# A router on the residual, first rows by a 0/1 matrix, and expert weights with buffers of their own

## The chip, the cores and the metric

One core of a Trainium2 chip runs the kernel. The metric is the device time of one execution in microseconds (us).

## What is computed

A backbone of two layers over 512 latent and 256 context tokens, 1024 wide, all in float32. Each layer: modulated RMSNorm, one input projection, three token mixers side by side, an output projection and a gated residual; then a modulated RMSNorm and a channel mixer, in the first layer a SwiGLU, in the last one the two best of eight experts:

```python
x = x + g1 * out_l
hl2 = modulate(rmsnorm(x, norm2[l]), sh2, sc2)
x = x + g2 * channel_mixer(hl2, l, ...)
...
probs = jax.nn.softmax((h @ router).astype(F32), axis=-1)
top_p, top_i = lax.top_k(probs, TOP_K)
top_p = top_p / jnp.sum(top_p, axis=-1, keepdims=True)
...
for e in range(N_EXPERTS):
    out = out + comb[..., e:e + 1] * swiglu(h, wg[e], wu[e], wd[e])
```

## The kernel before

Large products run in split float32: an operand is the sum of two parts (`hi`, `lo`, made by ACT at L206 and DVE at L207), and a product is three matmuls (`mm3`, L214 to L216, or `mm3x`, L220 to L222). Activations have features on partitions: `x[i]` is a [128, 512] tile, features 128 i and on, tokens along the row.

The order of the work is a static one for every engine: a scheduler walks over the program, and each engine runs its list in that order, waiting on semaphores. DMAs are issued from the lists of SP (weights), ACT and POOL; what waits at the head of a list holds what is behind it. SBUF is given out from two ends (`pa`, `pb`); a buffer over memory that another one had waits for that one's last reader. PSUM is shared out by name in `banks`.

What the change touches, all in the last layer:
- `tail`: loads the residual `xr0` to `xr7`, the gain row `g2p` and the router on ACT's queue (L617 to L623), and projects in two pieces of 256 tokens, token tiles 1 and 2 first, then 0 and 3. In a piece there are eight groups of 24 products of 256 columns, one for each 128 features, with a 512 KB weight tile (`wout`, four buffers) each; DVE adds each to the residual (L646). Then `stats` (L289) takes the mean square with products of a column of ones (L305) and a square root on DVE (`rsq`, L238 to L245: 12 dependent operations), a diagonal matrix `dg` times ones spreads it over the partitions (L316, L321), and the normalised tokens `hh` are x times that (DVE, L655) plus the shift (ACT, L656). Two modulation rows (`mod_rows`, L264 to L267, L662, L663) give `g2row`.
- `moe` (L757): router products on `hh` (L793), `tokens`: transposes (L230) of `hh` to rows `tk` and their store to DRAM (L798), then `route` (L948): the two best experts (`m`, `one`, `sel`), running counts (`cum`, `pos`), the 0/1 matrix `eq` (L989: which token is which of expert 0's rows), a search of the first expert's tokens by products with it (L994, L995), then `slots`, every token's rows, which are scattered to `ids` in DRAM and read back as `idx` (L807, L813).
- `Expert`: `prep` gathers an expert's rows `xa`, `xb` from DRAM (L1120, L1128), transposes and splits them; `run` makes ten steps of an expert, each with four weight tiles (`wmg`, `wmd`) that `load` has got a step ahead. Transposes of the residual to token rows stand ahead of the first expert. The weights have four buffers in `moe`'s first part and seven after `close()` has given the residual's memory back.
- `Combine` (from L839): puts the experts' rows on the residual and does the last norm, whose gain row is `nfrow`.

```python
        with tc.issue_after(found.ins):
            ex.first = ex.load((0, 0, None), 0)
        with tc.issue_after(placed.ins):
            tokens(x, True)
        close()
        ...
        k.weights(e2, None, pb, 7)
```

Of the kernel before, what the change touches and what calls it, by code (L numbers as in the profile page):

```python
# [8 lines left out]
F32 = mybir.dt.float32  # L9
# [11 lines left out]
# by layer: solve steps to a pair of query tiles; the step that the tokens' q and k are loaded at; how far ahead of the rest  # L21
# the solve goes; pairs behind every second chunk; buffers of L; work on one engine or another
# [5 lines left out]
# ---------------------------------------------------------------- host layout  # L28

def constants():  # L30
# [20 lines left out]
    # rotary tables of the latents, tokens on partitions  # L51
# [22 lines left out]
# features of a head of attention: the first of every rotated pair, then the second  # L74
# [3 lines left out]
# columns with features on partitions (12 tiles of 128), and with tokens on partitions (3 groups)  # L78
# [56 lines left out]
# ---------------------------------------------------------------- kernel  # L135

class K:
    def __init__(self, es, tc, A, out, dbg=None):
# [23 lines left out]
        # tokens' inputs to the experts, the token of every row of an expert, the experts' rows  # L162
# [17 lines left out]
    def banks(self, es, **n):  # L180
        """PSUM buffers by use, until es closes; [128, 512], names in capitals twice that."""
# [16 lines left out]
    def split(self, raw, n=1024):  # L198
        """The two parts, each exact in float32r, that a float32 operand is the sum of."""
# [24 lines left out]
    def transposes(self, srcs, w=128, m=128, b="pt"):  # L224
        """srcs [m, w] each -> side by side in one PSUM tile [w, m]."""
# [7 lines left out]
    def rsq(self, pool, v, sh, scale, eps, out, tag):  # L233
        """out = 1 / sqrt(v scale + eps): a first guess from the bits, three Newton steps."""
# [12 lines left out]
    # -- the modulation vectors, d on partitions: modc[l][:, s, t] for s = latent, context  # L247
# [7 lines left out]
    def mod_rows(self, l, g, b):  # L255
        """512 of the modulation vectors' columns; latent in the first row of every 32, context in the second."""
# [23 lines left out]
    def gains(self, l, which):  # L280
        """norm gain times (1 + scale): [128, 2, 8]."""
# [7 lines left out]
    def stats(self, pool, x, segs):  # L289
        """1 / rms of the token columns of segs, on all partitions, one PSUM tile each."""  # L290
# [43 lines left out]
    def modnorm(self, pool, hh, hl, x, s, o, n, gain, modc, sh0):  # L334
        """h = x * rstd * gain + shift, in parts, columns o .. o + n of stream s."""
# [1502 lines left out]
```

## Time and profile before

| | |
|---|---|
| time, median of 3 runs | 2198.43 us (2196.98 to 2198.94) |
| the profiled execution's span | 2199.0 us |
| TensorE (PE) busy | 2051.8 us, 93% |
| VectorE (DVE) busy | 1398.2 us, 64% |
| ScalarE (ACT) busy | 1013.7 us, 46% |
| GpSimd (POOL) busy | 157.3 us, 7% |
| last projection, gapless products | 1508.73 to 1560.2 us |
| first product of expert 0 | 1601.48 us |

A view by lines or a timeline names an instruction by its line, engine and tiles (out<-in) and shapes; behind it, in brackets, stands the idle time of that engine just ahead of it and what ended it (`<-DMA raw<-wmg`: the arrival of a weight tile). PEld is the loading of stationary operands, which runs beside PE. A matmul of plain float32 is counted as two rows (x2), and as x4 for two of them. The view by stretches gives busy time, the share of full TensorE clock that was granted (PEclk) and the share and rate of the DMA engines.

### The profile page before, as it was taken

The page shows a single profiled execution, that of the slowest core. Times are in us where ns is not written, and L with a number is a line of the kernel's source. Part 1 is how long each engine was busy: PE and PEld are TensorE (multiplying, and loading weights), DVE is VectorE, ACT ScalarE, POOL GpSimd, SP SyncE. Part 2 cuts the span into 40 slices and gives each one's busy share as a digit, 9 for nine tenths or more (in the row PEclk, how much of TensorE's full clock was granted, in tenths as well). Part 3 has the DMA queues.
Part 4 walks back from the last instruction along what each step waited for, and adds up shares of the span by engine and source line. Part 5 has one row for each costly group of instructions (what it writes and reads, how often), then busy time and mean ns, then how long its engine had stood idle before and what let it go on. Part 6 is the DMA issues. An engine that isn't in the chain of part 4 may idle for free. (4 is left out here: it accounts for less than half of the span.)

```text
span 2199.0 us, 33960 instructions
## 1 busy us (share of the span) xinstructions
PE 2051.8 (93%) x12562; PEld 1647.8 (75%) x12562; DVE 1398.2 (64%) x2736; ACT 1013.7 (46%) x1771; POOL 157.3 (7%) x226
## 2 busy tenths in 40 slices
PE   6999999989999999999989997898889999999995
PEld 2988766776788888888859875677667777777774
DVE  4859967765442424242366599787667788766776
ACT  3664386633322222222235534763455576555554
POOL 0000201100000000000000003120020000000010
PEclk9999999999999999999999999999989999999998
DMA  6332544053432325131343323116497799667683
GB/s 260 96 119 65 169 162 159 30 190 103 151 111 86 116 82 216 34 98 58 96 170 113 105 75 108 40 30 208 178 262 277 240 349 343 208 234 234 241 286 127
DMA packets 120755, 342.48 MB, mean 156 GB/s; under 512 B 13104, under 2 KB 34592, under 8 KB 120576
## 3 DMA queue, kind: packets, MB, share of 16 engines
q1 hardware_dynamic: 80064, 271.75, 36.8%
q0 software_dynamic: 15248, 49.97, 6.7%
q10 hardware_dynamic: 25264, 18.42, 2.7%
q8 instruction: 107, 1.75, 0.3%
q14 instruction: 72, 0.59, 0.1%
HBM read 304.95 MB, written 35.14 MB: 155 GB/s over the span
## 5 line engine op out<-in xcount | busy, mean ns | idle before, releaser
L206 ACT ACTIVATE hi<-raw 128x1024 fp32r<-128x1024 f32 (+3 forms) x444 | 427.1, 987 | 350.6 <-PE ps L215 245.1
L207 DVE TENSOR_TENSOR lo<-raw,hi 128x1024 fp32r<-128x1024 f32 (+3 forms) x444 | 495.3, 1135 | 123.4 <-ACT hi L206 108.4
L214 PE MATMUL ps<-hh,hi 128*128 128x512 f32 (+1 forms) x1040 | 355.5, 342 | 0.5 <-ACT hi L206 0.5
L215 PE MATMUL ps<-hl,hi 128*128 128x512 f32 (+1 forms) x1040 | 354.9, 341 | 0.0
L216 PE MATMUL ps<-hh,lo 128*128 128x512 f32 (+1 forms) x1040 | 354.3, 341 | 0.0
L214 PEld LDWEIGHTS ps<-hh,hi 128*128 128x128 f32 x1040 | 197.4, 190 | 27.1 <-ACT gh L1226 2.5
L215 PEld LDWEIGHTS ps<-hl,hi 128*128 128x128 f32 x1040 | 197.3, 190 | 23.8
L216 PEld LDWEIGHTS ps<-hh,lo 128*128 128x128 f32 x1040 | 197.2, 190 | 23.6
L222 PE MATMUL ps<-lo,xh 128*128 128x512 f32 (+1 forms) x384 | 151.4, 395 | 8.3 <-DVE lo L207 5.1
L220 PE MATMUL ps<-hi,xh 128*128 128x512 f32 (+1 forms) x384 | 147.3, 384 | 3.6 <-ACT hi L206 3.2
L1225 DVE TENSOR_TENSOR sg<-sg,ps 128x512 f32<-128x512 f32 (+1 forms) x44 | 24.4, 555 | 197.1 <-PE ps L216 197.1
L221 PE MATMUL ps<-hi,xl 128*128 128x512 f32 (+1 forms) x384 | 145.7, 379 | 0.0
L215 PE MATMUL ps<-gl,hi 128*128 128x256 f32 (+1 forms) x352 | 119.6, 340 | 0.0
L214 PE MATMUL ps<-gh,hi 128*128 128x256 f32 (+1 forms) x352 | 119.1, 338 | 0.0
L216 PE MATMUL ps<-gh,lo 128*128 128x256 f32 (+1 forms) x352 | 118.6, 337 | 0.0
L222 PEld LDWEIGHTS ps<-lo,xh 128*128 128x128 f32 x384 | 73.1, 190 | 35.7 <-DVE lo L207 15.8
L739 DVE SCALAR_TENSOR_TENSOR xr<-ps,modc,xr 128x512 f32<-128x512 f32 (+1 forms) x80 | 49.4, 617 | 72.5 <-PE ps L216 72.4
L220 PE MATMUL ps<-hi,hh 128*128 128x400 f32 (+2 forms) x272 | 90.9, 335 | 2.9 <-ACT hi L206 2.7
L221 PE MATMUL ps<-hi,hl 128*128 128x400 f32 (+2 forms) x272 | 87.8, 324 | 0.0
L222 PE MATMUL ps<-lo,hh 128*128 128x400 f32 (+2 forms) x272 | 87.7, 326 | 0.0
L220 PEld LDWEIGHTS ps<-hi,xh 128*128 128x128 f32 x384 | 73.4, 191 | 17.6 <-ACT hi L206 4.6
L221 PEld LDWEIGHTS ps<-hi,xl 128*128 128x128 f32 x384 | 73.1, 190 | 14.6
(557 smaller groups left out, 4144.4 us busy)
## 6 DMA issues: line engine op xcount, KB each, us to landing
raw<-wmg SPq DMA_DIRECT2D x176, 512.0 KB, 5.5
raw<-wmod SPq DMA_DIRECT2D x96, 512.0 KB, 4.6
raw<-wmd SPq DMA_DIRECT2D x80, 512.0 KB, 4.8
raw<-wgu SPq DMA_DIRECT2D x44, 512.0 KB, 3.9
raw<-wout SPq DMA_DIRECT2D x32, 512.0 KB, 3.8
raw<-wt SPq DMA_DIRECT2D x24, 512.0 KB, 3.6
raw<-wd SPq DMA_DIRECT2D x32, 256.0 KB, 2.7
raw<-wd SPq DMA_DIRECT2D x16, 384.0 KB, 3.1
```

The source lines that it names most:

```text
L206: self.nc.scalar.activation(hi, src, AF.Copy)
L207: self.nc.vector.tensor_sub(lo, src, hi.bitcast(F32))
L214: mm(out, wh, xh, start=start, stop=False)
L215: mm(out, wh, xl, start=False, stop=False)
L216: mm(out, wl, xh, start=False, stop=stop)
L220: mm(out, xh, wh, start=start, stop=False)
L221: mm(out, xl, wh, start=False, stop=False)
L222: mm(out, xh, wl, start=False, stop=stop)
L739: nc.vector.scalar_tensor_tensor(x[d][:, o:o + n], p[:, :n], k.modc[l][:, s, 40 + d:41 + d], x[d][:, o:o + n], op0=OP.mult, op1=OP.add)
L1225: nc.vector.tensor_mul(s, s, pu)
```

## The change

- Router on the residual. The norm's factor is the same for all of a token's features, so the router is multiplied with the gain once (`rg`, L649), applied to the residual as each group of the projection is done (`sums`, L668), and scaled by the factor behind it (L700); the shift's share is a constant of eight numbers (`lc`), by eight matmuls with a [128, 1024] copy of the shift (L651, L655). The sums of squares are products of one column (L670) of squares that ACT makes. `sums(m - 1)` stands behind group m.
- First expert's rows by products. The 0/1 matrix is kept (in `xa`, L1037), and `place` (L1163) multiplies the token rows `tk` with it: 32 float32 products of 192 columns give expert 0's rows with features on partitions. Gathers for expert 0, their transposes and the search are gone.
- Expert weights own their buffers: seven tiles, and `g2p`, opened ahead of the residual's at the end `pb`; the first seven tiles are loaded in the first piece of the projection (L686). The residual's transposes, `close()` and the load of `nfrow` are done in step 1 of expert 0; the copy of `g2row` is gone; the token rows are stored from ACT's queue (L841).

The diff, cut to its core:

```diff
 def tail(k, l, cat, mix, ec):
+    if last:
+        wm, g2p = pb(ec2, "wm", 7), pb(ec2, "g2")
     hp = pb(eh, "hp2")
...
-    k.banks(eb, ps=6, pn=2)
+    if last:
+        k.banks(eb, ps=4, pn=2, pl=2)
+    else:
+        k.banks(eb, ps=6, pn=2)
...
+        if last:
+            router = np_.tile([128, 8, 32], F32, name="router", bufs=1)
+            nc.scalar.dma_start(router, A["router"])
...
+            nc.vector.tensor_mul(rg, router, gain[:, 0].unsqueeze(2).to_broadcast([128, 8, 32]))
+            nc.vector.tensor_copy(shb, k.modc[l][:, 0, 24:32].unsqueeze(2).to_broadcast([128, 8, 128]))
+            for i in range(8):
+                nc.tensor.matmul(p[:, 0:8], shb[:, i], router[:, i, 0:8], start=i == 0, stop=i == 7)
+            nc.vector.tensor_copy(lc, p[:, 0:8])
...
+            def sums(m):
+                xs = cut(x[m], o, n)
+                sq = np_.tile([128, 256], F32, name="sq", bufs=3)
+                nc.scalar.activation(like(sq, o), xs, AF.Square)
+                j = 32 * (m % 4)
+                nc.tensor.matmul(pl[j:j + 32, :256], rg[:, m, :], xs, start=m < 4, stop=m >= 4, tile_position=(0, j))
+                for t in range(2):
+                    nc.tensor.matmul(pq[:, t:t + 1], sq[:, t * 128:t * 128 + 128], k.C("ones")[:, 0:1], start=m == 0 and t == 0, stop=m == 7,
+                                     skip_group_check=True)
...
+                if last and m:
+                    sums(m - 1)
+                if last and o == MID and m % 2:
+                    for r in range(m - 1, min(m + 1, 7)):
+                        raws.append(wm.tile([128, 1024], F32, name="raw"))
+                        nc.sync.dma_start(raws[-1], A["wmg"][0, r])
...
-                rs, = k.stats(np_, x, [(o, n)])
+                sums(7)
+                nc.vector.tensor_copy(lt, pl[:, :256])
+                k.rsq(np_, pq[:, 0:2], [128, 2], 1.0 / 1024, EPS, ss, "s")
+                for t in range(2):
+                    nc.tensor.matmul(pl[:, 256 + 8 * t:264 + 8 * t], lt[:, t * 128:t * 128 + 128], k.C("fold8"), start=True, stop=True)
+                nc.vector.tensor_mul(lg[:, o], pl[:, 256:272].rearrange("p (t e) -> p t e", t=2), ss.unsqueeze(2).to_broadcast([128, 2, 8]))
+                nc.vector.tensor_add(lg[:, o], lg[:, o], lc.unsqueeze(1).to_broadcast([128, 2, 8]))
...
 def moe(k, l, x, hs, g2row, close, lg, wm, raws):
-        k.weights(es, 8, pa, 4)
+        k.wraw, k.whl = wm, [pa(es, "w" + x, 8) for x in "hl"]
...
-            for t in range(4):
+            for t in (1, 2, 0, 3):
...
-                    nc.tensor.matmul(pl[j:j + 32, :256], k.router[:, i, :], hs[i][:, o:o + 256], start=i < 4, stop=i >= 4,
-                                     tile_position=(0, j))
...
-                nc.sync.dma_start(k.ht[t * 128:t * 128 + 128], tk[:, t])
+                nc.scalar.dma_start(k.ht[t * 128:t * 128 + 128], tk[:, t])
...
             ex.first = ex.load((0, 0, None), 0)
-        with tc.issue_after(placed.ins):
-            tokens(x, True)
-        close()
+            ex.place(tk, eq)
...
+        def residual():
+            tokens(x, True)
+            close()
+            cb.open(pb(e2, "cb"))
...
+    def place(self, tk, eq):
+        for q in range(4):
+            p = k.psum("pt")
+            for i in range(2):
+                f = (2 * q + i) * 128
+                for t in range(4):
+                    nc.tensor.matmul(p[:, i * CAP:i * CAP + CAP], tk[:, t, f:f + 128], eq[:, t], start=t == 0, stop=t == 3)
+            pv, f = p[:, :2 * CAP].rearrange("p (a t) -> p a t", a=2), slice(2 * q, 2 * q + 2)
+            k.parts(pv[:, :, 0:MAIN], xh[:, f], xl[:, f])
+            k.parts(pv[:, :, MAIN:], xs[:, f, 0:TAIL], xs[:, f, TAIL:])
```

The order on PE at the start of the last projection, after the change; `shb` is the copied shift, `pg` and `R,L` belong to the recurrence that the projection's last inputs come from, cat2 and cat3 are inputs of the projection:

```order
L230 MATMUL pg<-cst,oacc 128x128 x4
L1849 MATMUL pg<-R,L 64x64 x4
L655 MATMUL pn<-router,shb 128x8 x8
L214 MATMUL ps<-cat2h,hi 128x256
L215 MATMUL ps<-cat2l,hi 128x256
L216 MATMUL ps<-cat2h,lo 128x256
L214 MATMUL ps<-cat3h,hi 128x256
```

The products with the router now stand between the recurrence and the projection's products on cat2; before, those came behind the recurrence at once.

PE inside the projection. Before, around a pair of sums of squares, in the second piece's first group:

```order
L216 MATMUL ps<-cat7h,lo 128x256
L214 MATMUL ps<-cat2h,hi 128x256
L215 MATMUL ps<-cat2l,hi 128x256
L305 MATMUL pn<-sq,cst 32x256 x2
L216 MATMUL ps<-cat2h,lo 128x256
L214 MATMUL ps<-cat3h,hi 128x256
L215 MATMUL ps<-cat3l,hi 128x256
```

After, at the end of a group in the first piece (`xr` are residual tiles, `rg` the router times the gain, `sq` squares):

```order
L215 MATMUL ps<-cat1l,hi 128x256
L216 MATMUL ps<-cat1h,lo 128x256
L668 MATMUL pl<-xr_14317,rg 32x256
L668 MATMUL pl<-xr_14319,rg 32x256
L668 MATMUL pl<-xr_14321,rg 32x256
L668 MATMUL pl<-xr_14323,rg 32x256
L214 MATMUL ps<-cat5h,hi 128x256
L215 MATMUL ps<-cat5l,hi 128x256
L216 MATMUL ps<-cat5h,lo 128x256
L668 MATMUL pl<-xr_14325,rg 32x256
L670 MATMUL pn<-cst,sq 128x1 x2
L214 MATMUL ps<-cat6h,hi 128x256
```

Products of router and residual now stand in both pieces, four in a row here and one alone further on, and one-column products with the squares behind them.

DVE from the 0/1 matrix on. Before, the splits of expert 0's weights (`lo`) begin behind the search (`first`):

```order
L995 CAST first<-ps 128x1
L996 CAST first<-ps 64x1
L1011 TENSOR_TENSOR ex_15241<-ex_15240 128x8
L1061 TENSOR_SCALAR p_15094<-p_15094 128x4
L1065 TENSOR_TENSOR p_15216<-one_15190,pw 128x4
L1011 TENSOR_TENSOR ex_15242<-ex_15241 128x8
L207 TENSOR_TENSOR lo<-raw,hi 128x1024
L1011 TENSOR_TENSOR acc<-ex_15242 128x8
L1066 TENSOR_TENSOR pt_15095<-pt_15095,p_15216 128x4
```

After, just ahead of the first part of expert 0's rows (`xl<-pt`), which frees a PSUM buffer of `place`:

```order
L207 TENSOR_TENSOR lo<-raw,hi 128x1024
L1063 SCALAR_TENSOR_TENSOR pos<-cst,pos 128x32
L1087 TENSOR_SCALAR jb<-jb 128x8
L207 TENSOR_TENSOR lo<-raw,hi 128x1024
L1066 TENSOR_TENSOR lgt<-one_15231,pos 128x32
L1093 CAST jobs<-jb 128x9
L207 TENSOR_TENSOR lo<-raw,hi 128x1024
L1067 TENSOR_REDUCE row_15291<-lgt 128x4
L207 TENSOR_TENSOR xl<-pt,xh 128x256
```

These are the last three of six weight splits that DVE does between the matrix and the first part of the rows.

## Rows read from the trace of the kernel before

**Rows 1.** The page, busy time (us, share of the span) of each engine.
```profile
PE 2051.8 (93%) x12562; PEld 1647.8 (75%) x12562; DVE 1398.2 (64%) x2736; ACT 1013.7 (46%) x1771; POOL 157.3 (7%) x226
```

**Rows 2.** Stretches: us, busy us by engine (instructions), PEclk, DMA share, GB/s.
```profile
1490.00:1510.00 20.00, 13.96 (x145) 11.65 (x141) 18.87 (x52) 7.02 (x15) 1.23 (x2) 0.83 0.95 310
...
1530.00:1560.00 30.00, 29.76 (x226) 26.26 (x225) 18.65 (x41) 11.50 (x19) 0.00 (x0) 1.00 0.42 138
...
1590.00:1602.00 12.00, 6.53 (x29) 4.73 (x29) 8.01 (x30) 2.79 (x5) 7.09 (x7) 0.58 0.71 115
...
1602.00:1624.00 22.00, 17.68 (x64) 12.24 (x65) 9.86 (x11) 10.20 (x13) 3.88 (x5) 0.84 0.88 203
```

**Rows 3.** Timeline of PE, an insert: start us, us, instruction.
```profile
1533.08 0.28 PE L215 MATMUL ps<-cat2l,hi 128*128 128x256 f32 x1
...
1533.29 0.62 PE L305 MATMUL pn<-sq,cst 128*32 128x256 f32 x4
...
1533.84 0.39 PE L216 MATMUL ps<-cat2h,lo 128*128 128x256 f32 x1
```

**Rows 4.** Timeline of PE, the search for expert 0's tokens.
```profile
1584.37 1.61 PE L994 MATMUL ps<-cst,eq 128*128 128x1 f32 x16 [0.80 <-DVE eq L989]
```

**Rows 5.** Timeline of ACT's queue and PE; DMA issues of 1486:1512, KB each, us to landing.
```profile
1501.45 0.44 ACTq L623 DMA_DIRECT2D router<-router  x1
...
1508.73 0.28 PE L214 MATMUL ps<-cat3h,hi 128*128 128x256 f32 x1
...
raw<-wout SPq DMA_DIRECT2D x7, 512.0 KB, 5.8
...
router<-router ACTq DMA_DIRECT2D x1, 128.0 KB, 5.7
```

**Rows 6.** Timeline of PE and DVE behind the projection's last product.
```profile
1559.98 0.28 PE L216 MATMUL ps<-cat5h,lo 128*128 128x256 f32 x1
...
1566.33 2.24 PE L264 MATMUL ps<-raw,sT 128*32 128x512 f32 x8 [0.26 <-DMA raw<-wmod]
...
1566.69 0.17 DVE L238 TENSOR_SCALAR rqxs<-ss 128x2 f32<-128x2 f32 x1
...
1569.06 0.42 DVE L316 TENSOR_TENSOR dg<-cst,ss 128x256 f32<-128x256 f32 x1
...
1570.34 3.22 DVE L655 SCALAR_TENSOR_TENSOR hh<-xr,gain,pn 128x256 f32<-128x256 f32 x8 [0.86 <-PE pn L321]
...
1573.91 0.69 DVE L663 TENSOR_TENSOR g2p<-g2p,ps 128x512 f32<-128x512 f32 x1 [0.35 <-PE ps L662]
...
1581.39 0.17 DVE L977 TENSOR_TENSOR cum<-cum,sel 128x8 f32<-128x8 f32 x1
...
1583.36 0.95 DVE L989 TENSOR_TENSOR eq<-cst,p 128x768 f32<-128x768 f32 x1
```

**Rows 7.** Timeline of PE: step 5 of expert 0, expert 2's first product, its step 5.
```profile
1642.57 0.28 PE L220 MATMUL ps<-hi,xh 128*128 128x256 f32 x1
...
1748.70 0.39 PE L220 MATMUL ps<-hi,xh 128*128 128x512 f32 x1
...
1780.17 0.28 PE L220 MATMUL ps<-hi,xh 128*128 128x256 f32 x1
```

**Rows 8.** Timeline of DVE, PE and ACT between the matrix and expert 0.
```profile
1586.49 1.22 DVE L207 TENSOR_TENSOR lo<-raw,hi 128x1024 fp32r<-128x1024 f32 x1
...
1594.55 0.17 DVE L1038 CAST slots<-od 128x4 int32<-128x4 f32 x1
...
1595.37 4.78 PE L230 MATMUL pt<-cst,xr 128*128 128x128 f32 x20 [6.13 <-DVE tk L784]
...
1609.42 2.24 ACT L206 ACTIVATE hi<-raw 128x1024 fp32r<-128x1024 f32 x2 [4.92 <-DMA raw<-wmg]
```

**Rows 9.** Timeline of POOL: index load and gather for expert 1.
```profile
1616.35 0.96 POOL L813 DMA_DIRECT2D idx<-ids  x1 [11.55 <-DMA ids<-tid,slots]
...
1625.21 1.02 POOL L1120 DMA_INDIRECT xa<-ex,idx  x1 [7.17 <-DVE gl L207]
```

More of the change, by code (lines that the diff above doesn't have):

```diff
@@ L787, in moe @@
             hp = pa(e1, "h3")
[L788 to L795 removed]
             tokens(hs, False)
             for t in range(4):
[L798 to L800 removed]
+                nc.scalar.dma_start(k.ht[t * 128:t * 128 + 128], tk[:, t])
+            routing = route(k, hp, lg, slots, pw, jobs, last, ex.tl("xa", [128, 1024])[:, :4 * CAP].rearrange("p (t c) -> p t c", t=4))
+            found, eq = next(routing)
             placed = next(routing)
@@ L814, in moe @@
             nc.gpsimd.dma_start(idx[:TAIL, 1], rows[MAIN:])
-            ex.idx = [(first[:, 0:1], first[:TAIL, 1:2])] + [(idx[:, 0, e:e + 1], idx[:TAIL, 1, e:e + 1]) for e in range(1, 8)]
+            ex.idx = [None] + [(idx[:, 0, e:e + 1], idx[:TAIL, 1, e:e + 1]) for e in range(1, 8)]
         k.tap("slots", slots)
@@ L820, in moe @@
             ex.first = ex.load((0, 0, None), 0)
-        with tc.issue_after(placed.ins):
-            tokens(x, True)
-        close()
+            ex.place(tk, eq)
         e2 = ExitStack()
         pb = pools(k, l)[1]
-        k.weights(e2, None, pb, 7)
-        cb = Combine(k, pb(e2, "cb"), ex, tk, slots, pw, nfrow)
+        def residual():
+            tokens(x, True)
+            close()
+            cb.open(pb(e2, "cb"))
+        cb = Combine(k, ex, tk, slots, pw)
         flags = nc.values_load(jobs[0:1, 8:9], min_val=0, max_val=256 * NJOBS + 255)
-        ex.run([(e, e * CAP, (flags & (1 << e)) > 0) for e in range(8)], {(6, 1): lambda: cb.gathers(0), (6, 8): lambda: cb.others(0), (7, 1): lambda: cb.gathers(1), (7, 8): lambda: cb.others(1),
+        ex.run([(e, e * CAP, (flags & (1 << e)) > 0) for e in range(8)], {(0, 1): residual, (6, 1): lambda: cb.gathers(0), (6, 8): lambda: cb.others(0), (7, 1): lambda: cb.gathers(1), (7, 8): lambda: cb.others(1),
                   (7, 2): lambda: cb.last(*last), (7, 6): cb.place}, cb)
@@ L945, in far, with route @@
         self.finish()
-def route(k, pool, lt, slots, pw, jobs, first, last):
+def route(k, pool, lg, slots, pw, jobs, last, eq):
     nc = k.nc
     T_ = lambda n, s: pool.tile(s, F32, name=n)
-    p = k.psum()
-    for t in range(4):
-        nc.tensor.matmul(p[:, t * 8:t * 8 + 8], lt[:, t * 128:t * 128 + 128], k.C("fold8"), start=True, stop=True)
     sh = [128, 4, 8]
     i8 = k.C("iota8").unsqueeze(1).to_broadcast(sh)
-    lg, tmp, w8 = T_("lg", sh), T_("lgt", sh), T_("lgw", sh)
-    nc.vector.tensor_copy(lg, p[:, :32].rearrange("p (t e) -> p t e", t=4))
+    tmp, w8 = T_("lgt", sh), T_("lgw", sh)
     nc.vector.tensor_scalar(w8, i8, -1.0, 8.0, op0=OP.mult, op1=OP.add)
@@ L1085, in run @@
         w, self.first = self.first or self.load(*work[0]), None
-        self.prep(*jobs[0])
-        after = None
+        if not self.placed:
+            self.prep(*jobs[0])
+        self.placed, after = False, None
         for i, (j, c) in enumerate(work):
@@ L1101, in load @@
         if c < 6:
-            return [k.weight(sel(k.A["wmg"])[4 * c + r]) for r in range(4 if c < 5 else 2)]
+            return [k.split(self.raws.pop(0)) if self.raws else k.weight(sel(k.A["wmg"])[4 * c + r]) for r in range(4 if c < 5 else 2)]
         h, f0 = (c - 6) // 2, 6 * (c % 2)
```

70 lines of the change are left out of this document (38 added, 32 removed).

## The prediction

> **What bounds the kernel now.** I read the page first: TensorE (PE) is busy for 93% of the 2199.0 us span, so only PE's idle stretches and PE work that is added or dropped can change the time [rows 1]. Then the table of stretches. In 1530 to 1560, the second half of the last output projection, PE works 29.76 of 30 us [rows 2]. Behind it lies the passage: in 1590 to 1602 PE is busy 6.53 of 12 us and in 1602 to 1624 17.68 of 22, with granted clocks of 0.58 and 0.84 of full speed, 1.2 GHz and 2.4 GHz mixed [rows 2]. There the waits are read one by one. A second loose place is the start of the projection, 1490 to 1510: PE 13.96 of 20 us, DMA share 0.95 [rows 2].
>
> All sums are against the profiled execution, 2199.0 us; the median of the three runs is 0.6 lower. I call 0.2% (4.4 us) what a measurement can tell from no change: 2194.0 to 2202.8.
>
> **1. Sums and router products in the projection's stream: +9.3.** The projection's products follow each other every 0.12 us. An inserted pair of sums of squares costs more than its duration: the product ahead starts at 1533.08, the next one at 1533.84, so 0.64 goes to the insert, 0.55 of it from the insert's own start [rows 3]. Before, the first piece holds six such inserts, 6 x 0.64 = 3.84, and the second none, its sums come after its last product. After, sixteen router products of 256 columns (L668) and sixteen pairs of one-column sums (L670) go there.
> - One router product: the nearest row is that insert, of 256 columns in f32 too, 0.55. The search of before has products of one column, 16 rows in 1.61 us, 0.10 each [rows 4]; a pair of sums is 4 such passes, 0.40 behind another insert, 0.55 alone with the break.
> - First piece: four router products run together (0.7: two neighbours' four rows share 0.62 in [rows 3]), four apart (2.2); of the sums four stand alone (2.2), four beside a router product (1.6), and the two fold products add 0.55: 7.25. Less 3.84: +3.4.
> - Second piece: six router products in the stream (3.3) and sums behind them (2.55): +5.85.
> Bounds: if the one-column sums vanish under weight loads, +3; if nothing shares a break, 16 x 0.64 + 16 x 0.40 - 3.84 = +13.
>
> The trace has 0.10 for a pass of one column [rows 4]. The Trainium skill (TensorE: Matmul & The Clock Gate, section "Wait — 56ns, not 53.3ns?") gives a floor of about 25 ns from one matmul's start to the next, however few the columns. By it, an estimate, the 64 passes would take 1.6 us instead of 6.4, and the sum would be 4.8 lower; the row stands against it, and I keep the row.
>
> **2. The start of the projection: +4.** Eight new products (L655), ahead of all but six of the first group's products, need the router in SBUF. Its load is the last of ten on ACT's queue: issued at 1501.45, 5.7 us to landing, 1507.2 [rows 5]. Before, products go gapless at full clock from 1508.73 [rows 5]. After, four loads of expert weights of 512 KB each are issued in the same stretch, where the DMA engines are already 0.95 busy at 310 GB/s: 2 MB more is up to 6.7 us for what queues with it. I take the router at 1509.5, the eight products (16 passes of 0.10, some at the lower clock) to 1511.3, four products to be caught up, and about 1 us for products at 1.2 GHz behind the longer idle time (0.83 is granted on the mean of 1490 to 1510 as it is [rows 2]): +4. Bounds: 0 (the load lands as before, its products beside others) to +8. Queued behind the router on ACT's queue is nothing of PE's; DVE's multiplication of router by gain waits for the same load and holds the cat1 tiles a little.
>
> **3. From the last product to the 0/1 matrix: -4.5.** Before: the last product starts at 1559.98 (ends 1560.2), the matrix is made at 1583.36 + 0.95 = 1584.3 [rows 6]: 24.1. After, on the same clock: residual update 0.6, square 0.4, then PE has five products of the modulation row (0.28 each of 8 in 2.24 [rows 6]) and one router product ahead of the last sums: 1562.6. The square root's chain, 1566.69 to 1569.03 before [rows 6], is 2.4: 1565.0. One row update (0.69 [rows 6], behind L715's 1.13) stands in front of the diagonal in DVE's order: 1566.3; diagonal 0.4, its product 0.7, so the normalised tokens start at 1568.2 instead of 1570.34 [rows 6]. The router's products on the normalised tokens, their copies, the fold and its wait are gone. But the second row update now stands ahead of the running counts on DVE, and it waits for PE behind the first transposes, and those for ACT's shift of the tokens with a weight split of 1.05 among them: about 1576, against 1581.39 for the counts before [rows 6]. From there to the matrix 2.9 as before, and 0.8 for handovers that I can't price: 1579.8. Bounds -6 to -3.
>
> **4. From the matrix to the first expert at full pace: -3.** Before, expert 0's step 5 begins at 1642.57; expert 2, undisturbed, takes 1780.17 - 1748.70 = 31.5 for the same five steps [rows 7], so expert 0 in effect began at 1611.1, 26.8 behind the matrix. In that time stand the search (1.61 [rows 4] and a wait), the gather, residual transposes held by DVE (PE idle 6.13 [rows 8]), and ACT waiting for expert weights, 4.92 [rows 8]. After: 32 products of 192 columns, 64 passes at 0.20 (0.27 for 256 columns, half of an insert), 12.9, but only two PSUM buffers take them, and DVE's order puts six splits of 1.22 [rows 8] ahead of the first part that frees one: the third group waits till 10.2, the fourth about 2, and PE is at full pace at 17.3. The 32 transposes of the residual (20 in 4.78 at the low clock [rows 8], so some 0.14 each at the full one, 4.5, and hops) now stand inside step 1 of expert 0: +5. About 1.5 for the lower clock after PE's idle 3 us. Together 23.8: -3. The weights wait is gone, seven tiles being loaded ahead. Bounds: -8 (splits overlap with the products, no low clock) to +3.
>
> Removed at no gain: the copy of the gain row on ACT (ACT has spare time there), the gathers for expert 0 on POOL. Moved at no cost: token rows from SP's queue to ACT's, the reading of nfrow.
>
> Sum: +9.3 + 4 - 4.5 - 3 = +5.8, a profile of 2204.8, a median of 2204.
>
> **Rivals.**
> *Faster.* The small products cost little, since weight loads and products overlap (PEld is 26.26 busy of 30 us beside PE's 29.76 [rows 2]): term 1 at +3; the router lands early, term 2 at +1; and expert 0 begins without the low clock, term 4 at -5: 3 + 1 - 4.5 - 5 = -5.5, a median of 2193. It decides when an insert costs under 0.3 us. For it: four rows share one 0.62 [rows 3]. Against: each insert of before costs 0.64. 0.23.
> *No change.* Term 2 at 0 and the rest as summed: +1.8, 2200. The projection's cost is as large as the passage's gain. 0.27.
> *Slower still: expert 1's rows come late.* DVE finds the slots at 1594.55 [rows 8], 10 us behind the matrix; the index load begins only at 1616.35 and the gather at 1625.21 [rows 9]. After, the slots come 15 behind the matrix while expert 0 starts earlier: some 8 us of slack go. If that reaches the gather, expert 1 waits about 5: 2209. 0.10.
> *The loads ahead are not ahead.* The seven tiles lie where the mixers' buffers lay; the first waits for their last reader and stands on SP's queue ahead of the third weight tile of the projection. If it is released only at 1508, that tile lands at 1514 (5.8 to landing [rows 5]), is split by 1516.5, and PE stalls some 3 us more: 2207. 0.08.
>
> **Numbers.** The forecast, slower by the sum, has 0.32; with the last two rivals slower is 0.50, same 0.27, faster 0.23. Eight in ten: the low end reaches past the faster rival to 2190, the high end takes in the upper bound of term 2 with the late gather, 2213. The forecast's own range is 2203 to 2209.
>
> **What would show it.** The projection from its first gapless product to its last should take 9 us longer, each L668 opening about 0.64. L655 should wait for the router's load until about 1509.5. The tokens' normalisation should start 8 us behind the last product, the matrix end 19.6 behind it. L1163's third group should wait for DVE, and ACT should wait for no expert weights in expert 0. Wrong if an insert costs a third of this, or if expert 0's step 5 is not 55 us behind the matrix, as 23.8 + 31.5 has it.

## The result and the profile after

The changed kernel takes 2211.23 us (median of 9 runs, 2204.26 to 2216.82), the kernel before beside it 2198.94 (9 runs, 2193.72 to 2206.78): a ratio of 1.0053 [1.0036, 1.0069], the 95% interval in brackets, so it is slower by 0.5%, some 12 us. That is inside the wide range given, on the side that had the larger chance, 7 us above the number and outside the forecast's own range, 2203 to 2209. The profiled execution took 2208.62, with a span of 2207.0.

The page's first row, as in [rows 1], shows the loss already: PE has 11.5 us more of busy time and just as high a share.

```profile
PE 2063.3 (93%) x12638; PEld 1665.1 (75%) x12638; DVE 1392.2 (63%) x2737; ACT 1014.1 (46%) x1781; POOL 156.4 (7%) x224
```

Two executions don't reach the last layer's end at the same time, so I set all traces on one mark ahead of everything that the change moves: the start of ACT's second copy of `W` in the last step of the recurrence. In the kernel after it is this row of ACT's timeline; in the kernel before the same copy (at its L1746) starts at 1490.82, 3.0 us later.

```profile
1487.82 0.38 ACT L1805 ACTIVATE W<-pg 128x256 f32<-128x256 f32 x1 [0.49 <-PE pg L1801]
```

From that mark (A) to the projection's last product (P), from there to the 0/1 matrix (M, its start), and on to step 5 of expert 0 (S):

| us | A to P | P to M | M to S | A to S | forecast |
|---|---|---|---|---|---|
| before | 69.2 | 23.4 | 59.2 | 151.8 | |
| after | 90.3 | 18.1 | 54.0 | 162.3 | |
| difference | +21.1 | -5.3 | -5.3 | +10.5 | +13.3, -4.5, -3 |

Behind S both need the same time (2199.0 - 1642.57 = 556.4 before, 2207.0 - 1650.09 = 556.9 after). So the whole result is made here: the passage gained more than forecast, and the way to the last product lost 8 us more.

Where those 8 us are, the view by stretches says. Its columns are those of [rows 2].

```profile
1490.00:1500.00 10.00, 6.05 (x65) 4.83 (x60) 8.89 (x28) 3.53 (x7) 1.24 (x2) 0.76 0.99 361
1500.00:1510.00 10.00, 3.18 (x16) 2.58 (x16) 4.95 (x13) 2.72 (x5) 0.00 (x0) 0.67 1.02 350
1510.00:1520.00 10.00, 9.17 (x48) 8.83 (x49) 3.20 (x9) 0.28 (x1) 0.00 (x0) 0.54 0.54 195
```

In 1500 to 1510 PE, DVE and ACT all stand for half the time or more, while the DMA engines are full; in 1510 to 1520 PE works at nearly half clock. The timelines of SP's list, ACT and its list, and PE there, in order of time:

```profile
1490.56 0.80 SPq L686 DMA_DIRECT2D raw<-wmg  x2
1496.65 1.84 SPq L686 DMA_DIRECT2D raw<-wmg  x2
1497.15 8.00 ACTq L621 DMA_DIRECT2D xr<-xres  x4
1506.14 0.34 ACTq L645 DMA_DIRECT2D router<-router  x1
1506.53 2.00 ACT L206 ACTIVATE hi<-raw 128x1024 fp32r<-128x1024 f32 x2 [8.76 <-DMA xr<-xres]
1510.83 3.58 PE L655 MATMUL pn<-router,shb 128*128 128x8 f32 x16 [5.67 <-DMA router<-router]
1515.05 0.41 PE L214 MATMUL ps<-cat3h,hi 128*128 128x256 f32 x1
```

Four expert weight tiles (2 MB) are issued between 1490 and 1499. On ACT's list the last four `xr` loads then take 8.00 us to issue. Narrower windows of the same timeline show them one by one:

```profile
1500.29 0.33 ACTq L621 DMA_DIRECT2D xr<-xres  x1
1502.87 0.33 ACTq L621 DMA_DIRECT2D xr<-xres  x1
1504.82 0.33 ACTq L621 DMA_DIRECT2D xr<-xres  x1
```

An issue by itself is 0.33 us; the rest is waiting ahead of it. By the trace's semaphore events, the loads on SP's and ACT's lists take turns on eight semaphores in this stretch, and a load waits until the one that had its semaphore before has landed. The last three `xr` loads and the router's load meet the semaphores of the first four `xr` loads. Those were issued from 1493.38 to 1495.41, and their last events come at 1500.27, 1502.84, 1504.80 and 1506.12, each 0.02 to 0.03 us ahead of the issue that waited: 6.9 to 10.7 us to land.

The router's load is issued at 1506.14, 4.7 later than in [rows 5] though this execution is 3 us ahead. ACT's own next work, the weight split, stands behind both and has waited 8.76, until an `xr` load landed. PE waits 5.67 for the router. Then the clock is half: L655's sixteen passes take 3.58, and the products follow each other every 0.21 until 1519. From A, the first product on cat3h comes 27.2 behind, against 17.9 before (1508.73 in [rows 5]): +9.3, and about 2 more until the clock is full. Of the 21.1 us that A to P is longer, 5 are idle time of PE (11.6 us against 6.5); the rest is PE's own work, some of it at half clock.

The inserts, on PE's timeline (the columns of [rows 3]): a router product alone, a pair of sums alone, and both together.

```profile
1561.84 0.28 PE L216 MATMUL ps<-cat5h,lo 128*128 128x256 f32 x1
1562.05 0.62 PE L668 MATMUL pl<-xr,rg 128*32 128x256 f32 x2
1562.60 0.38 PE L214 MATMUL ps<-cat6h,hi 128*128 128x256 f32 x1
...
1563.41 0.28 PE L214 MATMUL ps<-cat2h,hi 128*128 128x256 f32 x1
1563.54 0.50 PE L670 MATMUL pn<-cst,sq 128*128 128x1 f32 x4
1563.90 0.36 PE L215 MATMUL ps<-cat2l,hi 128*128 128x256 f32 x1
...
1569.95 0.28 PE L216 MATMUL ps<-cat5h,lo 128*128 128x256 f32 x1
1570.16 0.62 PE L668 MATMUL pl<-xr,rg 128*32 128x256 f32 x2
1570.71 0.61 PE L670 MATMUL pn<-cst,sq 128*128 128x1 f32 x4
1571.18 0.36 PE L214 MATMUL ps<-cat6h,hi 128*128 128x256 f32 x1
```

Start to start less one product's 0.12 they cost 0.64, 0.37 and 1.11. From cat3h to the last product the stream takes 63.0 us against 51.25: +11.8. Added up insert by insert from the trace's starts, the new ones take 13.8 us and those of before 4.6 (the diagonal's product in both): +9.2. The half clock is about 1.9 of the rest, and products of the recurrence that now stand behind the first cat3h are 0.7.

The passage, on DVE's, PE's and ACT's timelines; they answer to [rows 6 to 8].

```profile
1578.08 0.28 PE L216 MATMUL ps<-cat5h,lo 128*128 128x256 f32 x1
1587.11 3.22 DVE L708 SCALAR_TENSOR_TENSOR hh<-xr,gain,pn 128x256 f32<-128x256 f32 x8
1594.17 0.16 DVE L1025 TENSOR_TENSOR cum<-cum,sel 128x8 f32<-128x8 f32 x1
1596.14 0.95 DVE L1037 TENSOR_TENSOR xa<-cst,p 128x768 f32<-128x768 f32 x1
1603.03 1.06 ACT L206 ACTIVATE hi<-raw 128x1024 fp32r<-128x1024 f32 x1 [4.54 <-DMA raw<-wmg]
1607.01 4.52 PE L1163 MATMUL pt<-xa,tk 128*128 128x192 f32 x16 [3.49 <-DVE lgt L1071]
1611.82 2.76 PE L1163 MATMUL pt<-xa,tk 128*128 128x192 f32 x16
1625.56 0.66 PE L230 MATMUL pt<-cst,xr 128*128 128x128 f32 x4 [2.10 <-DVE tk L835]
1650.09 0.28 PE L220 MATMUL ps<-hi,xh 128*128 128x256 f32 x1
```

The matrix ends 18.7 behind the last product's end (1578.36); `place`'s third group is held until 9.9 behind the matrix, and step 5 begins 53.0 behind it. The clock that was granted from the matrix to step 5 is not the same in the two traces: 0.97 of full speed here, 0.83 before. So a part of this gain came with the clock, and the traces don't price it apart.

### The profile page after: what moved, and what is told of

It reads as the page before. It is cut to its first block, busy times and chain, and to the rows that moved or that the text cites. A ratio compares the mean times of both kernels' runs of the same rounds, so it can differ in the third digit from the quotient of the medians.

```text
span 2207.0 us, 34138 instructions
## 1 busy us (share of the span) xinstructions
PE 2063.3 (93%) x12638; PEld 1665.1 (75%) x12638; DVE 1392.2 (63%) x2737; ACT 1014.1 (46%) x1781; POOL 156.4 (7%) x224
## 5 line engine op out<-in xcount | busy, mean ns | idle before, releaser
L222 PEld LDWEIGHTS ps<-lo,xh 128*128 128x128 f32 x384 | 72.6, 189 | 29.8 <-DVE lo L207 10.7
L793 DVE SCALAR_TENSOR_TENSOR xr<-ps,modc,xr 128x512 f32<-128x512 f32 (+1 forms) x80 | 49.3, 617 | 72.5 <-PE ps L216 72.4
L221 PE MATMUL ps<-hi,hl 128*128 128x400 f32 (+2 forms) x272 | 88.9, 328 | 0.0
```

The lines of the kernel that those rows point to most:

```text
L221: mm(out, xl, wh, start=False, stop=False)
L222: mm(out, xh, wl, start=False, stop=stop)
L793: nc.vector.scalar_tensor_tensor(x[d][:, o:o + n], p[:, :n], k.modc[l][:, s, 40 + d:41 + d], x[d][:, o:o + n], op0=OP.mult, op1=OP.add)
```

## The experiments

Two readings of the extra loss were open: the new work itself (L655 and the inserts, PE time wherever they stand), or the loads (weight tiles that come early hold the `xr` and router loads up, and with them ACT's list). The passage had a question of its own: is `place` bound by DVE's order? The table has the result, and from each trace the parts of the sum as above, PE's idle time from A to P, and the granted clock from M to S; what each shows is told under its heading.

| | median | ratio to before | A to P | PE idle, A to P | P to M | M to S | PEclk, M to S | A to S less 151.8 |
|---|---|---|---|---|---|---|---|---|
| before | | | 69.2 | 6.5 | 23.4 | 59.2 | 0.83 | 0 |
| the change | 2211.23 | 1.0053 [1.0036, 1.0069] | 90.3 | 11.6 | 18.1 | 54.0 | 0.97 | +10.5 |
| lc_late | 2210.01 | 1.0038 [1.0022, 1.0053] | 86.7 | 8.2 | 18.1 | 53.9 | 0.97 | +6.9 |
| no_traffic | 2209.27 | 1.0043 [1.0026, 1.006] | 89.4 | 12.1 | 18.1 | 53.9 | 0.97 | +9.7 |
| sums4 | 2207.76 | 1.0034 [1.0018, 1.005] | 85.1 | 12.4 | 21.6 | 54.8 | 0.94 | +9.7 |
| place2 | 2212.02 | 1.0048 [1.0033, 1.0063] | 89.5 | 11.8 | 18.1 | 54.7 | 0.94 | +10.4 |
| pool_x | 2207.43 | 1.0042 [1.0026, 1.0057] | 88.9 | 10.6 | 18.1 | 52.2 | 0.97 | +7.3 |
| late_wm | 2200.82 | 1.0010 [0.9999, 1.0021] | 85.0 | 6.7 | 18.1 | 50.0 | 1.00 | +1.2 |
| pool_q | 2203.83 | 1.0018 [1.0007, 1.0028] | 81.7 | 4.3 | 18.1 | 51.2 | 0.97 | -0.7 |
| best_a | 2199.70 | 1.0006 [0.9994, 1.0018] | 77.1 | 4.6 | 19.1 | 49.9 | 1.00 | -5.7 |
| no_ahead | 2211.41 | 1.0052 [1.0037, 1.0067] | 90.1 | 11.1 | 18.1 | 55.2 | 0.94 | +11.7 |
| best_b | 2196.57 | 1.0004 [0.9993, 1.0015] | 76.3 | 4.4 | 18.5 | 54.8 | 0.94 | -2.2 |
| best_c | 2201.92 | 1.0008 [0.9997, 1.0019] | 74.2 | 5.5 | 21.4 | 54.9 | 0.94 | -1.2 |
| old_router | 2196.18 | 0.998 [0.9966, 0.9993] | 70.3 | 6.2 | 25.1 | 48.1 | 0.99 | -8.3 |

Medians of different rows stand beside different runs of the kernel before (2198.0 to 2200.6), so the ratios are what is compared. A trace is one execution, and a profile can be several us off its kernel's median: best_a's was the shortest of its 11 runs, so that its -5.7 stands beside a ratio of 1.0006.

M to S goes with the clock granted there: 48 to 50 us at 0.99 and 1.00, 51 to 54 at 0.97, about 55 at 0.94. Yet apart from place2 and old_router no run changes the engines' work behind the matrix. The views by stretches of late_wm and best_b, M to S:

```profile
1592.31:1642.27 49.96, 45.31 (x232) 37.31 (x231) 36.80 (x83) 25.43 (x41) 12.08 (x12) 1.00 0.80 254
1581.66:1636.48 54.82, 48.56 (x233) 40.12 (x231) 36.91 (x83) 25.73 (x41) 12.32 (x12) 0.94 0.73 236
```

So a difference of some us in that column is not put down to an edit here.

### The constant moved away (lc_late)

```diff
-            p = k.psum("pn")
-            for i in range(8):
-                nc.tensor.matmul(p[:, 0:8], shb[:, i], router[:, i, 0:8], start=i == 0, stop=i == 7)
-            nc.vector.tensor_copy(lc, p[:, 0:8])
...
                 sums(7)
+                if o == MID:
+                    pc = k.psum("pn")
+                    for i in range(8):
+                        nc.tensor.matmul(pc[:, 0:8], shb[:, i], router[:, i, 0:8], start=i == 0, stop=i == 7)
+                    nc.vector.tensor_copy(lc, pc[:, 0:8])
```

> The change with the eight products L655 (shift times router) taken out of the start of the projection and done at the end of its first piece. Theory A (the wait at the start is theirs alone): PE goes on with the products on cat2 at about 1506 instead of 1514.3, the 3.58 us of L655 become about 1.7 at full clock later, so the projection's last product ends 6 to 8 us earlier than 1578.2 and the time falls by 6 to 8. Theory B (the load of the router holds more than PE: DVE's router times gain waits for it too, and what stands behind it on DVE makes the cat1 parts): PE stops again a few products later, until about 1511, and less than 3 us is won. Theory C (traffic of the loads ahead holds the weight tiles): PE waits for ACT's or DVE's splits of wout, under 3 us won.

By the ratios 0.15% (3 us) came back, in the trace 3.6, not the whole loss; the two intervals overlap, so the time alone doesn't show the gain. ACT's stand is as long as ever, and reaches PE by another way: DVE's half of the weight split waits 4.87 for ACT's, the recurrence's sum `oacc` stands behind it on DVE's list, and PE waits 2.45 for that. At full clock L655's products (here L692) take 1.85 instead of 3.58. ACT's, DVE's and PE's timelines:

```profile
1512.16 2.00 ACT L206 ACTIVATE hi<-raw 128x1024 fp32r<-128x1024 f32 x2 [8.96 <-DMA xr<-xres]
1513.25 1.23 DVE L207 TENSOR_TENSOR lo<-raw,hi 128x1024 fp32r<-128x1024 f32 x1 [4.87 <-ACT hi L206]
1515.05 1.12 PE L1850 MATMUL pg<-R,L 128*64 128x64 f32 x8 [2.45 <-DVE oacc L1856]
1523.28 1.85 PE L692 MATMUL pn<-router,shb 128*128 128x8 f32 x16
```

### The early tiles asked for in the second piece (no_traffic)

```diff
-                if last and o == MID and m % 2:
+                if last and o == ENDS and m % 2:
```

> The change with the seven early expert tiles loaded in the projection's second piece instead of the first, all else as it is. If the 2 MB beside the residual's loads are what brings the router late (my term 2), the router is in SBUF at about 1507 to 1508 instead of 1510.8 and the time falls by 3 to 4. If the router is late by its place, the last of ten loads on ACT's queue, it still lands at about 1510 and the time stays within 1 us. Behind the projection nothing should change: the tiles are there before 1580 either way.

It took nothing away: SP's timeline has `1492.14 8.12 SPq L686 DMA_DIRECT2D raw<-wmg  x4`. The buffers are free, so the order lets the loads go early wherever they stand in the program. Nothing follows on either reading.

### Sums in fours (sums4)

The inserts stand together, four router products and then four tiles' sums at a time:

```diff
-                if last and m:
-                    sums(m - 1)
+                if last and m == 4:
+                    sums(range(4))
...
-                sums(7)
+                sums(range(4, 8))
```

> The change with the sums and router products taken in fours (after the fifth group and after the last) instead of one group at a time. If a lone router product costs 0.64 because it stands alone in its column group, and every insert has a break, four cost about 0.7 together and the projection's stream shortens by 5 to 6 us; some 1 to 1.5 of it is given back behind the last product, where four pairs of sums now stand instead of one: time -4 to -5. If the sums cost their passes (0.10 each) wherever they stand and there is no break to share, only the router products gain: -2 to -3.

By the ratios 0.19% (4 us) came back, as expected, though the intervals overlap here too. The stream is 5.2 shorter, as fewer breaks would have it. Behind the last product 3.5 of that is given back, but not by the four tiles' sums: DVE begins the square root 3.8 us behind the last product in this trace as in the change's. In this trace the clock falls there (0.76 granted from P to M); best_a has the same sums in the same place at full clock and gives back 1.0, best_b 0.4. The stretches P to M of sums4 and best_a:

```profile
1573.10:1594.66 21.56, 19.96 (x99) 9.24 (x97) 12.78 (x60) 13.58 (x24) 0.00 (x0) 0.76 0.38 131
1565.93:1585.00 19.07, 16.59 (x99) 8.10 (x97) 12.58 (x60) 13.47 (x24) 0.00 (x0) 1.00 0.43 148
```

### Fewer splits ahead of the rows (place2)

DVE makes two weight splits ahead of the first part of the rows instead of six; the others follow the groups one by one:

```diff
-            ex.first = ex.load((0, 0, None), 0)
-            ex.place(tk, eq)
+            ex.first = [k.split(raws.pop(0)) for _ in range(2)]
+            rows_ = ex.place(tk, eq)
+            at = next(rows_)
+        for q in range(3):
+            with tc.issue_after(at.ins):
+                if q < 2:
+                    ex.first.append(k.split(raws.pop(0)))
+                at = next(rows_)
...
```

> The change with DVE's order between the 0/1 matrix and expert 0 changed: two weight splits ahead of the first part of expert 0's rows instead of six, the others between and behind the parts. If DVE's order is what stops PE for 3.49 us ahead of the third group of L1163, that wait goes under 1 us, the third group runs at full clock (2.8 instead of 4.5), and expert 0's step 5 comes 3 to 4.5 us earlier against the matrix. Rival: the products of step 0 then wait for the splits that were put off, and expert 0's step 5 comes at the same 53 us behind the matrix.

The third group (here L1176) comes on at full clock and waits 2.35 instead of 3.49, and the residual's transposes wait 3.19 in exchange. PE's timeline:

```profile
1609.68 5.44 PE L1176 MATMUL pt<-xa,tk 128*128 128x192 f32 x32 [2.35 <-DVE xs L207]
1629.81 1.12 PE L230 MATMUL pt<-cst,xr 128*128 128x128 f32 x4 [3.19 <-ACT tk L835]
```

The time is the change's, and M to S is not the 3 to 4.5 us shorter that was expected. The wait moves. M to S had 0.94 of the clock here and 0.97 in the change, so a gain of a microsecond or two could hide; that what ACT and DVE have to do ahead of step 5 is the limit was not shown.

### The loads on POOL's list (pool_x), and the router first (pool_q)

```diff
-        nc.scalar.dma_start(t, k.xsrc[l][:, i, :w])
+        (nc.gpsimd if last else nc.scalar).dma_start(t, k.xsrc[l][:, i, :w])
...
-            nc.scalar.dma_start(router, A["router"])
+            nc.gpsimd.dma_start(router, A["router"])
```

pool_q gives the router a place in `g2p`'s memory besides, and issues its load ahead of all of `tail`'s.

> The change with the loads of the residual and the router issued from POOL's list instead of ACT's. In the change's trace ACT stands for 8.76 us in front of a weight split because the loads ahead of it in its list wait for earlier loads to land, and the cat0 parts stand behind. Theory D: with ACT free, its splits are made at once and PE waits only for L655, whose router now comes by POOL's list; the projection's last product ends 5 to 8 us earlier against its first product on cat6 (85.1 in the change), and the time falls by 5 to 8. Theory A (only L655's wait for the router counts): the router lands as late as before, last of nine loads, and under 2 us is won.

> As the run with the loads on POOL's list, and the router's load the first of them, its tile beside the gain row. Nothing at the start of the projection then waits for the router: L655 runs in PE's idle time there. Theory D: the last product ends 8 to 10 us earlier against the first product on cat6 than in the change (about 76 instead of 85.1), time -8 to -10. If PE stops at the start for something else (the recurrence, the weight tiles' traffic), it wins no more than the run with the residual's loads on POOL's list alone.

pool_x frees ACT's list, and ACT no longer stands for a load; yet L655 waits as long. The router's load is issued at 1499.44 and ends PE's wait at 1509.07, 9.6 later, with the DMA engines full in that stretch. POOL's and PE's timelines and the view by stretches:

```profile
1499.44 0.54 POOL L645 DMA_DIRECT2D router<-router  x1 [2.08 <-DMA go_z<-z]
1509.07 3.58 PE L655 MATMUL pn<-router,shb 128*128 128x8 f32 x16 [5.59 <-DMA router<-router]
```

```profile
1500.00:1510.00 10.00, 4.28 (x19) 3.99 (x19) 3.52 (x7) 0.00 (x0) 0.00 (x0) 0.50 1.03 399
```

In pool_q the router is there early: L655 waits 0.31, for the copied shift, and A to P is 8.6 shorter than in the change. By the ratios the time falls by 0.35% (8 us). PE's timeline:

```profile
1504.38 3.58 PE L655 MATMUL pn<-router,shb 128*128 128x8 f32 x16 [0.31 <-DVE shb L651]
```

So another list alone does little, and an early router with it does much. L655 still takes 3.58, at half clock; PE has waited 3.08 for a weight split just ahead of it.

The Trainium skill (DMA: Bandwidth & Descriptors, "Issuing engines are not separate DMA queues") says that DMAs from ACT, SP and POOL run on the same 16 engines, and that another issuer saves its sequencer's time only, usually little. pool_x agrees: the DMA engines are as full with another issuer, and what that issuer won is 0.11%, not clear of noise. ACT's 8.00 us were not the time of issuing, 0.33 a load, but waits for earlier loads to land.

### The early tiles held back (late_wm)

The seven loads of expert weights wait on SP's list for the second piece's `wout` tiles (`k.at` is the weight load issued last):

```diff
-                if last and o == MID and m % 2:
-                    for r in range(m - 1, min(m + 1, 7)):
+                if last and o == ENDS and m < 7:
+                    with tc.issue_after(k.at.ins):
                         raws.append(wm.tile([128, 1024], F32, name="raw"))
-                        nc.sync.dma_start(raws[-1], A["wmg"][0, r])
+                        nc.sync.dma_start(raws[-1], A["wmg"][0, m])
```

> The change with the seven expert tiles held back in SP's list until the weight tiles of the projection's second piece, so that none of them is in flight at its start. If the loads ahead are what makes the residual's loads late (their traffic, and that ACT's loads wait for earlier ones to land), ACT's stand of 8.76 falls under 4, the router lands 3 us earlier, and the time falls by 3 to 6. If ACT stands because ten loads are in its list whatever else is in flight, stand and time stay within 1.5 us. Behind the projection: same as the change.

The largest single step: 0.43% against the change by the ratios, some 9 us, and no difference from the kernel before that can be told. SP's, ACT's and PE's timelines:

```profile
1489.24 32.77 SPq L195 DMA_DIRECT2D raw<-wout  x9
1498.59 2.00 ACTq L621 DMA_DIRECT2D xr<-xres  x4
1500.62 0.46 ACTq L645 DMA_DIRECT2D router<-router  x1
1501.41 2.00 ACT L206 ACTIVATE hi<-raw 128x1024 fp32r<-128x1024 f32 x2 [2.20 <-issue]
1506.54 3.58 PE L655 MATMUL pn<-router,shb 128*128 128x8 f32 x16 [0.70 <-DMA router<-router]
```

The same four `xr` loads are issued in 2.00 us instead of 8.00, ACT waits 2.20 instead of 8.76, PE 0.70 instead of 5.67. By the trace's semaphore events the eight `xr` loads land 4.1 to 6.2 us behind their issue, and no issue on ACT's list waits for one of them. A to P is 5.3 shorter, and 4.9 of that is idle time of PE. More than the 3 to 6 us expected came back: M to S is 4.0 shorter too, since no half clock falls on `place`'s third group and the residual's transposes don't wait; that part may be one execution's.

### The early loads taken out, the buffers kept (no_ahead)

```diff
-                if last and o == MID and m % 2:
-                    for r in range(m - 1, min(m + 1, 7)):
-                        raws.append(wm.tile([128, 1024], F32, name="raw"))
-                        nc.sync.dma_start(raws[-1], A["wmg"][0, r])
```

> The change without the seven early loads: expert 0's tiles are loaded by its own steps, into the seven buffers that they now own. Theory D (the tiles in flight at the start hold the residual's loads, and those hold ACT): the projection's stretch is that of the run with the tiles held back (79.8 from the first product on cat6 to the last product, against 85.1), and the time is about 2201. If the early loads are what wins the passage, expert 0 now waits for weights as before, and its step 5 comes 5 to 10 us later behind the matrix (50 with the tiles held back); if the buffers of their own are enough, it comes within 2 us of that.

The time is that of the change. The expert's ordinary loads (L195) go just as early by themselves, and ACT stands as before. SP's and ACT's timelines:

```profile
1493.32 8.41 SPq L195 DMA_DIRECT2D raw<-wmg  x4
1509.71 2.01 ACT L206 ACTIVATE hi<-raw 128x1024 fp32r<-128x1024 f32 x2 [9.11 <-DMA xr<-xres]
```

So it is the buffers of their own that set the loads free, not the lines that ask for them.

### Putting the mends together (best_a, best_b, best_c)

best_a is pool_q with sums4; best_b is late_wm, pool_q and sums4; best_c is late_wm, lc_late and sums4.

> The loads on POOL's list with the router first, together with the sums in fours. If the two costs are separate terms of the sum, they add: -8 to -10 and -3.5 (the measured median of the fours against the change), about -12 in all, so 2199, no different from the kernel before; if the passage's own gain of 10 us (matrix to expert 0, less the projection) is then all that is left, it lands up to 3 us below it. Rival: both shorten the same stretch (the start runs into the same DMA traffic) and the sum is -9 at most.

> Tiles held back, the residual's loads and first of all the router's on POOL's list, sums in fours. If the start, L655's wait and the inserts are separate terms: 2201 with the tiles held back, less 3.5 for the fours, less 3 to 4 for L655 at half clock behind its wait: 2194 to 2196, below the kernel before by 2 to 5. If the start was one cost, paid once, whichever way it is taken out (tiles held back, or loads on POOL's list), it is the 2199.7 of the run with POOL's list and the fours, within 2.

> Tiles held back, the eight products L655 at the end of the first piece, sums in fours; loads on ACT's list as in the change. Against the run with the loads on POOL's list this tells whether POOL's list is needed once the tiles are held back: if ACT stands only because of the tiles, this gives the same 2194 to 2197; if ACT still stands in front of its splits for over 3 us, 2 to 4 more.

None differs from the kernel before by a measurable amount. All three have lost the wait for the router: A to P is 74 to 77, and 5 to 8 longer than before, about what grouped inserts (9.2 less 5.2) and L655 (1.85 or 3.58) take. The mends don't add up: best_b's ratio is best_a's within noise, and PE still stands once in each, for a weight split in best_a (3.08) and best_c (4.22), for the copied shift in best_b (3.51, where pool_q alone had 0.31).

### The router's part undone (old_router)

late_wm with statistics, router and PSUM shares as before the change (products on `hh`, L793 then); own buffers, late loads and `place` stay:

```diff
-                sums(7)
...
+                rs, = k.stats(np_, x, [(o, n)])
...
+                for i in range(8):
+                    j = 32 * (i % 4)
+                    nc.tensor.matmul(pl[j:j + 32, :256], k.router[:, i, :], hs[i][:, o:o + 256], start=i < 4, stop=i >= 4,
+                                     tile_position=(0, j))
```

> The run with the tiles held back, with the change's first part undone: sums of squares and router products as in the kernel before (behind the norm, on the normalised tokens), own buffers and expert 0's rows by products kept. Theory D: the projection loses the inserts of the change (9 us by my sum, 10 as traced) and L655 with its half clock (about 5), so from the first product on cat6 to the last it takes 65 to 67 instead of 79.8; the matrix comes 23 to 25 behind the last product instead of 18; in all 6 to 9 less than the 2200.8 of the tiles held back, 2192 to 2195, faster than the kernel before by 3 to 6. Rival: the router on the residual pays for itself behind the projection, and undoing it gives nothing: 2199 to 2202.

The ratio is 0.998 [0.9966, 0.9993]: faster than the kernel before, by about 0.2%, and the lowest of all that were run, though its interval touches best_b's. A to P is back within 1.1 of before. The matrix comes 7.0 later behind the last product than in late_wm, with the router's products on PE again:

```profile
1563.46 0.28 PE L216 MATMUL ps<-cat5h,lo 128*128 128x256 f32 x1
1576.36 4.27 PE L801 MATMUL ps<-hh,router 128*32 128x256 f32 x32 [0.26 <-ACT hh L666]
1588.53 0.95 DVE L1006 TENSOR_TENSOR xa<-cst,p 128x768 f32<-128x768 f32 x1
1636.63 0.28 PE L220 MATMUL ps<-hi,xh 128*128 128x256 f32 x1
```

So the router on the residual shortens the wait behind the last product by 7 and pays 14.7 for it ahead of it (85.0 - 70.3): against late_wm, by the ratios, it loses 0.3%, some 6 us. In its mended forms it breaks even from A to the matrix: best_a, best_b and best_c pay 6.8, 6.0 and 3.9 and get back 6.0, 6.6 and 3.6. Their ratios are 0.24% to 0.28% above old_router's all the same; what lies between is not shown. What gained is behind the matrix, where `place` and the own buffers stand: M to S is 11.1 shorter than before, and PE is idle for 2.7 us of it instead of 13.3. The two were not run apart, and the clock granted there, 0.99 against 0.83, has a share that was not measured.

## Why the prediction was right, and where it was off

That the kernel is slower, and by a gain of the passage that is less than the cost ahead of it, came as said. That the time falls inside the wide range is in part luck: its high end, 2213, was the upper bound of term 2 (+8) together with a late gather for expert 1 (5 us). Term 2 went beyond its bound, and the gather was not late for anything.

**Term 1, the inserts (+9.3): right.** +9.2, added up in the trace. An insert of 256 columns opens 0.64 as said. A pair of one-column sums alone costs 0.37 (0.55 said) and both together 1.11 (0.95 said); these two misses cancel. A pass of one column takes 0.12 to 0.13 here, as sums4's twelve rows in one run have it (`1573.87 1.50 PE L673 MATMUL pn<-cst,sq 128*128 128x1 f32 x12`); the row that was kept had 0.10. The Trainium skill (TensorE: Matmul & The Clock Gate, "Wait — 56ns, not 53.3ns?") gives a floor of about 25 ns from one matmul's start to the next; the passes here take five times that.

**Term 2, the start of the projection (+4): the term that failed.** It was about +12 (21.1 less the inserts' 9.2). Three sentences were wrong. "Queued behind the router on ACT's queue is nothing of PE's" looked only at PE: the load's issue stands on the list on which ACT computes, and the weight split and the parts of cat0 and cat1 are behind it. The 2 MB were counted as a delay of the router's landing alone; what they delayed first was the landing of the `xr` loads, for which the later issues on ACT's list waited, so the router was issued 7.7 later from the same mark. It ended PE's wait at 1510.8, said 1509.5, in an execution 3 us ahead. And L655 was priced at 1.8 and took 3.58, at half clock; behind it the clock stayed half for another 4 us of the stream.

late_wm tells the parts apart. Without the stand PE's idle time from A to P is 4.9 less, nearly that of the kernel before. What is left of term 2 there is still +6.6 (85.0 less 69.2 and 9.2): L655 takes the same 3.58 behind a wait of only 0.70, and half clock follows it. So the wait was missing in the sum, and L655 with its half clock was priced too low besides.

**Term 3, to the matrix (-4.5): right, a little small.** -5.3. The order was as worked out: less the 18.1 by which the last product is later, `hh` starts at 1569.0 (1568.2 said) and the counts at 1576.1 (1576 said).

**Term 4, to expert 0 (-3): right mechanism, mis-sized.** -5.3. The third group is held until 9.9 behind the matrix (10.2 said) and the fourth ends 17.5 behind it (17.3 said). Full pace to step 5 was priced at 38.0 (31.5, 5 and 1.5) and took 35.5, though the residual's transposes with their wait made 6.1 of it (5 said). No half clock falls into this part; it falls on the third group, ahead of it. Step 5 came 53.0 behind the matrix, not 55. That ACT would wait for no expert weights was wrong, 4.54 once, but PE shows no wait for it.

**The rivals.** "Faster" fell with the inserts' price. "Loads not ahead" named the right loads in the wrong place: they came earlier than thought, not later. Expert 1's late rows didn't come: slots are out at 1613 and the gather runs at 1641.47, but PE's longest wait from 1650 to 1730 is 0.3.

Together the misses, +8 in term 2 and -3 in terms 3 and 4, make the +10.5 of the trace out of +5.8; the measured ratio, 12 us, says about the same.

## What to carry to other kernels

A buffer of its own for a load is also leave to start early: ask what the load will then run beside, and put a floor under its start. A DMA that is issued from a computing engine's list delays that engine's work when the issue has to wait, here for an earlier load's landing, so read what is behind it on that list, for all engines. Moving small products off a dependent chain into a dense stream pays only if the chain they shorten is worth more than their breaks: here 7 us for 14.7, and about even up to the matrix with all mends. Before a stretch of one trace is held against another's, hold their granted clocks against each other.

## What was not expected of the hardware

Four issues of 256 KB loads on ACT's list took 8.00 us with four expert weight tiles issued beside the projection's, 2.00 without those. The waits are spread over the issues (2.8, 2.3 and 1.6 us between them, 1.0 ahead of the router's), and each ended with the landing of an earlier `xr` load.

A router load of 128 KB took 9.6 us to landing at 399 GB/s (pool_x), 5.7 before at 309.

The mark A lay between 1486.5 and 1497.3 us in the fourteen traces, though the engines' work ahead of it is the same in all but for a few loads. What makes that spread was not looked into, nor how much of the difference between single traces and medians (5.8 us for best_a) it is.
